# Mixer B of a two-layer encoder: one more dense step ahead of the first transposes, query transposes ahead of the next logits, inverse roots item by item

## The chip, the cores and the metric

The kernel runs on one core of a Trainium2 chip. The metric is the device time of one execution in microseconds (us); the time of a kernel is the median of its runs. Engines are named as the profile names them: PE is TensorE (PEld its weight loads), DVE VectorE, ACT ScalarE, POOL GpSimd, SP SyncE, which here issues most DMAs.

## What is computed

A trunk of two layers over 512 tokens of width 1024. Each layer projects its input once into everything it needs (8448 columns), runs two attention branches, A and B, and merges them. The change is in branch B: grouped attention with 8 query heads and 2 key heads of 64, whose queries and keys are scaled by an inverse root of their mean square and then rotated.

```python
def rms_head(x, g):
    y = xf * lax.rsqrt(jnp.mean(xf * xf, axis=-1, keepdims=True) + QK_EPS) * g
...
def mixer_b(q, k, v, q_norm_g, k_norm_g):
    q = axial_rope(rms_head(q, q_norm_g), ang_row, ang_col)
    k = axial_rope(rms_head(k, k_norm_g), ang_row, ang_col)
    ...
        logits = jnp.einsum('bqkge,bske->bkgqs', qblk, k) * (HEAD_DIM ** -0.5)
        p = jax.nn.softmax(logits, axis=-1)
        return jnp.einsum('bkgqs,bske->bqkge', p, v)
```

Each layer ends with two output projections, a gated sum, one more projection and a layer norm. Everything is float32; dense products are made of three products of rounded parts (high by high, high by low, low by high).

## The kernel before

**The order of the program.** Every engine runs its own instructions in the order in which the program emits them, so the order is written by hand. Per layer there are two generators: `main` (preparation and mixer B, then mixer A, lines 1320 to 1326) and `fill` (all remaining dense products, lines 1328 to 1332). `weave` (line 857) alternates them: each `yield 1` of `main` gives 1.1 credits, and each whole credit lets `fill` emit one dense step. A dense step is either half of a 128x512 output tile (12 matmuls of 512 columns, `feature_unit`) or one 128-token block (24 matmuls of 256 columns, `token_mms`). After each dense step `tick` runs jobs that have come due (`run_later`) and splits one piece of a later weight chunk into its parts: a rounding copy on ACT (line 175) and a subtraction on DVE (line 176).

**Mixer B.** It has 16 items per layer, each two heads of one 128-query block. For item i, `pipeline` (line 671) emits:

- `Q(i)`: two PE transposes of the rotated queries into a PSUM bank (line 616), a copy of the high part on ACT (line 618) and a subtraction for the low part on DVE (line 619).
- `L(i)`: four PE matmuls that make 128x1024 logits (line 632), a maximum on DVE (line 634), a small multiplication by the query factors (line 637), two exponentials on ACT (line 640), a reciprocal and two scalings on DVE (lines 642 and 644).
- `T(i)`: eight PE transposes of the scaled exponentials (line 666) and an eviction of 128x1024 on ACT (line 668).
- `V(i)`: 16 matmuls with the values and a copy on DVE (line 658).

Before the loop come `Q(0)`, `Q(1)`, one `yield 1`, `L(0)` and two times `yield 1`. In the loop the order is `T(i)`, `L(i+1)`, `Q(i+2)`, a yield, `V(i)`, a yield. Mixer A uses the same `pipeline` with `Q` set to None.

**The inverse roots of the queries.** `b_steps` (line 565) calls `q_sums` four times per layer, for (ch, rp) = (0,0), then (0,1) and (1,0) one after the other, then (1,1): squares on ACT (line 475) and a sum on DVE (line 476) into 8 of 32 columns of the tile `qn`. After the fourth, `q_roots` calls `first_root` for all 32 columns: one DVE instruction (line 479), and a power of -1/2 on POOL (line 480). The keys use the same function on 8 columns (tile `nst`). At the first `L`, `q_factors` (line 555) corrects all 32 roots by five small DVE instructions (lines 507 to 510 and 560); the maximum of `L(0)` is emitted behind them.

**PSUM.** Four banks "b" are handed out first in, first out (`B1`). Each dense output tile, each `Q` and each `V` takes one; the next user's first matmul waits until the eviction of the former one is done. In layer 0 the job `rows_` (line 418), which fills two banks from `b<-g,g` matmuls and evicts them on ACT (line 423), and then `bias_rows` (line 251) come due in the tick of the last dense step before `T(0)`. The banks are taken there in the order 3 and 0 (`rows_`), 1 (`bias_rows`), and the dense tile of that step has bank 2.

Of the kernel before, what the change touches and what calls it, by code (L numbers as in the profile page):

```python
# [38 lines left out]
def trunk_kernel(ctx, tc, x, c, rel_table, ln_g, ln_b, w_ada, b_ada, w_in, b_gate,  # L39
# [432 lines left out]
    def square_sums(xq, v):  # L472

        sq = tmp4("s")
        act.activation(sq[:, 0:512], xq, AF.Square)
        dve.tensor_reduce(out=v, in_=sq[:, 0:512].rearrange("p (g d) -> p g d", d=64), op=ADD, axis=AX.X)

    def first_root(v, y):
        dve.tensor_scalar(v, v, 1.0 / 64, 1e-6, op0=MUL, op1=ADD)
        pool.tensor_tensor(out=y, in0=v, in1=mhalf.to_broadcast([128, v.shape[1]]), op=OP.pow)  # L480
# [43 lines left out]
    def k_rotate(st):  # L524

        kn = st["kn"] = small.tile([128, 3, 8], F32, tag="nst", name=fresh("nst"))
        square_sums(st["xk"], kn[:, 0])
        first_root(kn[:, 0], kn[:, 1])
        (a_, b_), sq = rope_parts(st["xk"], 4, 2, 0, 1)
        st["km"] = sq[:, 0:512].rearrange("p (r h d) -> p r h d", r=4, d=64)  # L530
        dve.tensor_add(st["km"], a_, b_)
        G.put(st["xk"])

    def k_scale(st):

        v, y, t = (st["kn"][:, j] for j in range(3))
        newton(v, y, t)
        for rp in range(2):
            kd = st["kd", rp] = G.get()
            kdv = kd.rearrange("p (r h e d) -> p r h e d", r=2, h=2, e=2)  # L540
            for r2 in range(2):
                r = 2 * rp + r2
                dve.tensor_tensor(out=kdv[:, r2], in0=st["km"][:, r, :, None, :].to_broadcast([128, 2, 2, 64]),
                                  in1=y[:, 2 * r:2 * r + 2][:, :, None, None].to_broadcast([128, 2, 2, 64]), op=MUL)

    def q_sums(st, ch, rp):
        if "qn" not in st:
            st["qn"] = small.tile([128, 3, 32], F32, tag="qn", name=fresh("qn"))
        at = 16 * ch + 8 * rp
        square_sums(st["xq", ch, rp], st["qn"][:, 0, at:at + 8])  # L550

    def q_roots(st):
        first_root(st["qn"][:, 0], st["qn"][:, 1])

    def q_factors(st):
        if "qf" not in st:
# [5 lines left out]
    def q_rotate(st, ch, rp):  # L562
        st["qd", ch, 2 * rp], st["qd", ch, 2 * rp + 1] = rope_q(st.pop(("xq", ch, rp)), 2 * rp)

    def b_steps(st):

        k_rotate(st)
        yield
        k_scale(st)
        q_sums(st, 0, 0)  # L570
        yield
        b_keys(st)
        q_rotate(st, 0, 0)
        yield
        q_sums(st, 0, 1)
        q_sums(st, 1, 0)
        yield
        while ("xq", 1, 1) not in st:
            yield
        q_sums(st, 1, 1)  # L580
        q_roots(st)

    def b_prepare(st, rest):
        for _ in st["steps"]:
# [10 lines left out]
    def b_keys(st):  # L595
        for kv in range(2):
            o = B1.get()
            for r in range(4):
                k = st["kd", r // 2].rearrange("p (r h f) -> p r h f", r=2, h=2)[:, r % 2, kv]
                pe.transpose(o[:, 128 * r:128 * r + 128], k, idn)  # L600
            ks = G.get(F32R)
            act.activation(ks, o, AF.Copy)
            dve.tensor_tensor(out=ks[64:128], in0=o[64:128], in1=ks[64:128].bitcast(F32), op=SUB)
            B1.put(o)
            st["ks", kv] = ks
        G.put(st["kd", 0], st["kd", 1])

    def mixer_b(st, ys):
# [41 lines left out]
        def V(i):  # L650
# [8 lines left out]
            B1.put(o)  # L659

        yield from pipeline(len(subs), Q, L, T, V, lambda i: True, st["more"])

    def transpose_p(p):
# [7 lines left out]
    def pipeline(n, Q, L, T, V, need, more=()):  # L671
        if Q:
            Q(0)
            if n > 1:
                Q(1)
        yield 1
        while not need(0):
            yield "need"
        L(0)
        yield 1  # L680
        yield 1
        for i in range(n):
            T(i)
            if i + 1 < n:
                while not need(i + 1):
                    yield "need"
                L(i + 1)
            if Q and i + 2 < n:
                Q(i + 2)
            yield 1  # L690
            V(i)
            if more:
                more.popleft()()
            yield 1
# [5 lines left out]
    def mixer_a(st, hf, ys, more=()):  # L700
# [90 lines left out]
        def need(i):  # L791
            k, pr, pp = subs[i]
            return all(("k", g, hf, pr) in st for g in ((1, 2) if k else (0,)))

        yield from pipeline(len(subs), None, L, T, V, need, more)
        for h in range(4):
            G.put(st.pop(("b0", hf, h)))
# [491 lines left out]
    for l in range(DEPTH):  # L1289
        st = {"more": deque()}  # L1290
        st["steps"] = b_steps(st)
        if l == 0:
            start_layer0(st)
# [107 lines left out]
```

## Time and profile before

| | us |
|---|---|
| median of three runs | 1209.2 (1207.27 to 1209.75) |
| the profiled execution | 1208.29 |
| its span, from the first to the last instruction | 1206.5 |
| PE busy | 1164.3 |
| DVE busy | 674.6 |
| ACT busy | 530.9 |
| POOL busy | 51.6 |

Times in the rows count from the start of the span. Mixer B lies at about 70 to 240 us in layer 0 and 645 to 820 us in layer 1. The profile's granted clock is 1.00 where TensorE runs at 2.4 GHz and 0.5 where it runs at 1.2 GHz.

### The profile page before, as it was taken

What the parts mean: (1) busy time and instruction counts of PE and PEld (TensorE: products, weight loads), DVE (VectorE), ACT (ScalarE), POOL (GpSimd) and SP (SyncE); (2) the same over time, 40 slices, a digit from 0 to 9 for tenths busy, and PEclk for the clock granted to TensorE, in tenths of its full rate; (3) what the DMA queues carried; (4) which work ended last, traced back from release to release, by engine and by line L of the source; (5) the groups of instructions that cost most, each with busy time, mean ns of one, the idle gap of its engine ahead of it and who ended that gap; (6) DMA issues with size and microseconds to landing.
All of it is one profiled execution on the core that took longest, in us unless ns stands there. A gap on an engine that the chain in (4) does not pass through costs nothing.

```text
span 1206.5 us, 19164 instructions
## 1 busy us (share of the span) xinstructions
PE 1164.3 (97%) x7491; PEld 996.7 (83%) x7491; DVE 674.6 (56%) x1576; ACT 530.9 (44%) x1112; POOL 51.6 (4%) x79
## 2 busy tenths in 40 slices
PE   6889999999999999999989899999999999999996
PEld 6878888888887787888989788888888778888896
DVE  6776665555455355336755566754433532943477
ACT  2355545444454454323374445444544454532320
POOL 0021000001000000000001001001000000000000
PEclk9999999999999999999999999999999999999998
DMA  9934434446352233234422335435332322333331
GB/s 280 285 115 135 139 96 127 130 140 176 109 155 88 70 122 105 90 103 154 163 73 71 95 102 152 139 93 177 102 100 67 106 72 94 123 99 102 125 106 70
DMA packets 161314, 146.31 MB, mean 121 GB/s; under 512 B 8942, under 2 KB 149078, under 8 KB 161224
## 3 DMA queue, kind: packets, MB, share of 16 engines
q1 hardware_dynamic: 159176, 139.71, 37.8%
q0 software_dynamic: 2048, 5.38, 1.9%
q8 instruction: 59, 0.97, 0.3%
q14 instruction: 31, 0.25, 0.1%
HBM read 134.87 MB, written 8.62 MB: 119 GB/s over the span
## 4 chain that ended last, share of the span: by engine, by line
PE 83%; DVE 8%; ACT 3%; DMA 2%; issue 1%; SPq 1%; POOL 1%; DVEq 0%; ACTq 0%
PE b L90 71%; PE L L90 6%; PE T L666 5%; DMA raw<-in_w_ada_dram 2%; DVE acc L283 1%; POOL qn L480 1%; DVE wl L176 1%; PE T L90 1%; DVE bst L634 0%; ACT s L640 0%; ACT g L951 0%; PE b L616 0%; DMA s<-in_w_in_dram 0%; SPq L1002 0%; DVE g L1255 0%
## 5 line engine op out<-in xcount | busy, mean ns | idle before, releaser
L176 DVE TENSOR_TENSOR wl<-raw,wh 128x512 fp32r<-128x512 f32 x304 | 205.6, 687 | 296.7 <-ACT wh L175 296.7
L90 PE MATMUL b<-uh,wh 128*128 128x512 f32 x768 | 309.8, 403 | 0.8 <-ACT wh L175 0.5
L90 PE MATMUL b<-uh,wl 128*128 128x512 f32 x768 | 299.6, 390 | 1.0 <-DVE wl L176 0.8
L90 PE MATMUL b<-ul,wh 128*128 128x512 f32 x768 | 300.0, 391 | 0.0
L175 ACT ACTIVATE wh<-raw 128x512 fp32r<-128x512 f32 x304 | 180.1, 623 | 32.7 <-issue 24.8
L90 PEld LDWEIGHTS b<-uh,wh 128*128 128x128 f32 x768 | 144.1, 188 | 42.6 <-issue 12.0
L90 PEld LDWEIGHTS b<-uh,wl 128*128 128x128 f32 x768 | 144.2, 188 | 33.0 <-DVE wl L176 1.8
L90 PEld LDWEIGHTS b<-ul,wh 128*128 128x128 f32 x768 | 144.3, 188 | 26.7
L90 PE MATMUL b<-wh,uh 128*128 128x256 f32 x416 | 122.0, 293 | 0.5 <-DVE qst L619 0.5
L90 PE MATMUL b<-wl,uh 128*128 128x256 f32 x416 | 118.0, 284 | 0.0
L90 PE MATMUL b<-wh,ul 128*128 128x256 f32 x416 | 117.7, 283 | 0.0
L668 ACT ACTIVATE pt<-T 128x1024 f32<-128x1024 f32 x64 | 65.4, 1021 | 79.9 <-PE T L666 79.9
L741 ACT ACTIVATE s<-s,ast 128x256 f32<-128x256 f32 x128 | 63.5, 498 | 78.0 <-DVE ast L736 73.9
L283 DVE SCALAR_TENSOR_TENSOR acc<-raw,sc,acc 128x256 f32<-128x256 f32 x168 | 81.3, 484 | 9.7 <-DMA raw<-in_w_ada_dram 4.6
L90 PEld LDWEIGHTS b<-wh,uh 128*128 128x128 f32 x416 | 79.9, 192 | 5.3 <-issue 3.2
L90 PEld LDWEIGHTS b<-wl,uh 128*128 128x128 f32 x416 | 80.1, 192 | 0.1
L90 PEld LDWEIGHTS b<-wh,ul 128*128 128x128 f32 x416 | 80.0, 192 | 0.0
L90 PE MATMUL b<-g,wh 128*128 128x512 f32 x256 | 79.2, 390 | 0.0
L666 PE MATMUL T<-idn,s 128*128 128x128 f32 x512 | 67.2, 274 | 7.2 <-DVE s L644 6.5
L90 PE MATMUL b<-wh,g 128*128 128x256 f32 x384 | 71.4, 284 | 0.7 <-DVE g L1194 0.5
L640 ACT ACTIVATE s<-L,bst,qn 128x512 f32<-128x512 f32 x64 | 49.3, 774 | 51.1 <-DVE bst L637 51.0
L666 PEld LDWEIGHTS T<-idn,s 128*128 128x128 f32 x512 | 59.1, 141 | 13.9 <-DVE s L644 7.2
(177 smaller groups left out, 1610.8 us busy)
## 6 DMA issues: line engine op xcount, KB each, us to landing
raw<-in_w_in_dram SPq DMA_DIRECT2D x126, 512.0 KB, 4.2
raw<-in_w_ada_dram SPq DMA_DIRECT2D x96, 256.0 KB, 3.5
raw<-in_w_o_dram SPq DMA_DIRECT2D x16, 512.0 KB
g<-in_x_dram SPq DMA_DIRECT2D x16, 256.0 KB, 5.9
vph<-g SPq DMA_DIRECT2D x16, 256.0 KB, 2.1
g<-vph SPq DMA_DIRECT2D x16, 256.0 KB, 5.7
g<-frow SPq DMA_DIRECT2D x32, 128.0 KB, 3.2
raw<-in_w_pa_dram SPq DMA_DIRECT2D x8, 512.0 KB, 3.4
```

The lines of the kernel that those rows point to most:

```text
L90: pe.matmul(o, l, r, start=start, stop=stop, skip_group_check=True)
L175: act.activation(hi[:, d], raw[:, s], AF.Copy)
L176: dve.tensor_sub(lo[:, d], raw[:, s], hi[:, d].bitcast(F32))
L283: dve.scalar_tensor_tensor(a, raw[:, k], col, a, op0=MUL, op1=ADD)
L480: pool.tensor_tensor(out=y, in0=v, in1=mhalf.to_broadcast([128, v.shape[1]]), op=OP.pow)
L640: act.activation(p[:, 512 * e:512 * e + 512], lg[:, 512 * e:512 * e + 512], AF.Exp, scale=f[:, e:e + 1], bias=sm[:, 0, e:e + 1], accum_out ...
L666: pe.transpose(t[:, 128 * j:128 * j + 128], p[:, 128 * j:128 * j + 128], idn)
L668: act.activation(pt, t, AF.Copy)
L741: act.activation(p4[:, e, b], p4[:, e, b], AF.Exp, bias=sm[:, e, b:b + 1], accum_out=s_t[:, rb, e, 1:2])
```

## The change

Three edits. In `pipeline`, a kernel with a `Q` (mixer B alone) yields three times instead of twice between `L(0)` and `T(0)`, and `Q(i+2)` is emitted between `T(i)` and `L(i+1)` instead of behind `L(i+1)`. In `q_sums`, `first_root` is called for the 8 columns just summed, so four times per layer on 8 columns instead of once on 32; `q_roots` goes.

```diff
         square_sums(st["xq", ch, rp], st["qn"][:, 0, at:at + 8])
-
-    def q_roots(st):
-        first_root(st["qn"][:, 0], st["qn"][:, 1])
+        first_root(st["qn"][:, 0, at:at + 8], st["qn"][:, 1, at:at + 8])
...
         q_sums(st, 1, 1)
-        q_roots(st)
...
         L(0)
-        yield 1
-        yield 1
+        for _ in range(3 if Q else 2):
+            yield 1
         for i in range(n):
             T(i)
+            if Q and i + 2 < n:
+                Q(i + 2)
             if i + 1 < n:
                 while not need(i + 1):
                     yield "need"
                 L(i + 1)
-            if Q and i + 2 < n:
-                Q(i + 2)
             yield 1
             V(i)
```

## Rows read from the trace of the kernel before

**Rows 1.** The page, busy time, share of the span and instructions of each engine.
```profile
PE 1164.3 (97%) x7491; PEld 996.7 (83%) x7491; DVE 674.6 (56%) x1576; ACT 530.9 (44%) x1112; POOL 51.6 (4%) x79
```
**Rows 2.** Waits of PE over the span: total us, times, longest us.
```profile
PE T L666 <- DVE s L644: 6.5, 2, 4.4
...
PE b L90 <- DVE qst L619: 0.8, 3, 0.4
```
**Rows 3.** Timeline of PE, layer 1: start us, us, what, idle before and releaser.
```profile
662.00 0.28 PE L90 MATMUL b<-wh,uh 128*128 128x256 f32 x1
...
664.88 0.28 PE L90 MATMUL b<-wh,uh 128*128 128x256 f32 x1
...
667.63 0.28 PE L90 MATMUL b<-wh,ul 128*128 128x256 f32 x1
672.34 1.53 PE L666 MATMUL T<-idn,s 128*128 128x128 f32 x8 [4.43 <-DVE s L644]
...
676.37 0.28 PE L90 MATMUL b<-wh,uh 128*128 128x256 f32 x1
```
**Rows 4.** Windows in layer 1: length, busy us by engine, granted clock, DMA.
```profile
666.00:672.00 6.00, 1.91 (x16) 1.71 (x15) 2.60 (x9) 3.35 (x7) 0.13 (x1) 1.00 0.00 0
672.00:676.00 4.00, 3.66 (x15) 3.17 (x16) 2.29 (x5) 2.12 (x4) 0.00 (x0) 0.61 0.38 115
```
**Rows 5.** Timeline of PE, layer 0, around the first transposes.
```profile
80.43 0.39 PE L90 MATMUL b<-uh,wh 128*128 128x512 f32 x1
...
83.15 0.39 PE L90 MATMUL b<-uh,wh 128*128 128x512 f32 x1
...
87.59 0.27 PE L255 MATMUL b<-idn,g 128*128 128x128 f32 x1
89.92 1.09 PE L666 MATMUL T<-idn,s 128*128 128x128 f32 x8 [2.06 <-DVE s L644]
...
91.92 0.47 PE L90 MATMUL b<-uh,wh 128*128 128x512 f32 x1
```
**Rows 6.** Timeline of DVE, layer 1, before, during and after the power on POOL.
```profile
654.79 1.27 DVE L476 TENSOR_REDUCE qn<-s 128x8 f32<-128x512 f32 x2
...
661.33 0.68 DVE L176 TENSOR_TENSOR wl<-raw,wh 128x512 fp32r<-128x512 f32 x1
666.16 0.19 DVE L507 TENSOR_TENSOR qn<-qn 128x32 f32<-128x32 f32 x1 [4.15 <-POOL qn L480]
```
**Rows 7.** Groups of POOL by line and shape: xcount, busy us, mean ns, idle before.
```profile
L480 POOL TENSOR_TENSOR qn<-qn,mhalf 128x32 f32<-128x32 f32 x2 | 10.9, 5428 | 25.2 <-DVE qn L479 25.2
...
L480 POOL TENSOR_TENSOR nst<-nst,mhalf 128x8 f32<-128x8 f32 x2 | 4.1, 2029 | 34.9 <-DVE nst L479 34.9
```
**Rows 8.** Timeline of DVE, layer 0, the last sums and the first correction.
```profile
75.49 1.27 DVE L476 TENSOR_REDUCE qn<-s 128x8 f32<-128x512 f32 x2
...
77.28 0.68 DVE L476 TENSOR_REDUCE qn<-s 128x8 f32<-128x512 f32 x1
...
83.72 0.19 DVE L507 TENSOR_TENSOR qn<-qn 128x32 f32<-128x32 f32 x1 [2.16 <-POOL qn L480]
```
**Rows 9.** Timeline of ACT, layer 0, behind the exponentials of L(0).
```profile
90.04 1.05 ACT L423 ACTIVATE g<-b 24x512 f32<-24x512 f32 x2
```
**Rows 10.** Timeline of ACT, layer 1, an eviction of T.
```profile
692.73 1.03 ACT L668 ACTIVATE pt<-T 128x1024 f32<-128x1024 f32 x1 [2.89 <-PE T L666]
```
**Rows 11.** All copies of line 618 on ACT: xcount, shortest, median, longest ns, first, last.
```profile
L618 ACT ACTIVATE qst<-b x32: 369/378/383, 76.7 to 800.1; 128x256 fp32r<-128x256 f32 x32
```
**Rows 12.** Timeline of DVE: a maximum and a subtraction (layer 1), scalings (layer 0).
```profile
693.59 1.23 DVE L634 TENSOR_REDUCE bst<-L 128x2 f32<-128x1024 f32 x1 [1.37 <-PE L L90]
...
697.79 0.42 DVE L619 TENSOR_TENSOR qst<-b,qst 128x256 fp32r<-128x256 f32 x1
...
183.83 0.88 DVE L644 TENSOR_SCALAR s<-s,bst 128x512 f32<-128x512 f32 x2
```
**Rows 13.** Timeline of PE, layer 0, the transposes that follow those scalings.
```profile
185.64 1.04 PE L666 MATMUL T<-idn,s 128*128 128x128 f32 x8
```

## The prediction

> **What bounds the kernel now.** I read the shares of busy time first: PE is busy in 97% of the span [rows 1], so an edit pays only where PE stands still or runs slowly. The waits of PE tell where that is [rows 2]. The longest entry is the transposes of line 666 waiting for the scaling of line 644: 6.5 us in two places. The three waits for line 619 are dense tiles whose bank was still held by a Q, 0.8 us together. The rest of the argument is the two places of the first entry, which the timeline of PE shows: in layer 1 PE ends its dense step at 667.91 and starts T(0) at 672.34, 4.43 us later [rows 3]; in layer 0 it stands for 2.06 us before 89.92 [rows 5].
>
> The layer-1 gap costs more than its length. Ahead of it the granted clock is 1.00, and in the 4 us after it 0.61, so part of that stretch ran at the lower level [rows 4]. From T(0) to the fourth dense matmul behind it took 676.37 - 672.34 = 4.03 us [rows 3]. The same T, L and Q took 91.92 - 89.92 = 2.00 us in layer 0 [rows 5], and three dense matmuls of 256 columns take 3 x 0.12 (2.88 us for 24 of them [rows 3]), together 2.36. So the slow clock costs 1.67 us. After the 2.06 us in layer 0 no such slowing is seen.
>
> What is late in both places is one chain: power on POOL, five corrections on DVE, maximum, exponentials, scaling, T. In layer 1 DVE stood 4.15 us for the power [rows 6], in layer 0 2.16 [rows 8].
>
> **The roots by items.** The power took 5.43 us on 32 columns and 2.03 on 8 [rows 7]; each layer gets four of the latter. In layer 1 the second and third sums end at about 655.4 and 656.1 [rows 6], so their powers take POOL from about 655.7 to 659.8; the fourth then starts where the long one did, 5.43 before 666.16, at 660.7. The chain gets shorter by 5.43 - 2.03 = 3.40 us, and T(0)'s data is ready at 672.34 - 3.40 = 668.94. In layer 0 POOL is a queue: the second, third and fourth sums end at about 76.2, 77.1 and 78.6 [rows 8], with the added DVE instruction of some 0.2 us behind each; the second power starts at about 76.45, the third and fourth wait for it, and the last ends at 76.45 + 3 x 2.03 + 0.05 = 82.6. The correction began at 83.72 [rows 8], so the gain there is only 1.1 us: data ready at 88.8. The three added DVE instructions a layer cost PE nothing: DVE waits for POOL behind them. Behind the powers on POOL nothing is due until the bias loads, tens of microseconds later; SP's queue isn't passed.
>
> In the long power of layer 1, DVE's subtraction of line 176, with two inputs in SBUF, took 0.68 us and ended at 662.01, when POOL still had 4 us to go [rows 6, 7]. The Trainium skill (SBUF — State Buffer, section Who interferes with whom) says that such a DVE instruction and a GpSimd instruction that reads SBUF exclude each other for the whole instruction. By that, with POOL at work without a break in layer 0, the subtraction ahead of the correction would start only when the last power ends, the correction 0.7 us later, and the whole gain would be 6.6 us instead of 7.3. The trace doesn't agree, so I take 7.3.
>
> **One more dense step.** The step is moved, not added: fill has one step less later. In layer 1 it is 24 matmuls of 256 columns, 664.88 - 662.00 = 2.88 us [rows 3]. It is the second half of a tile whose bank is already taken, and its weights were split before L(0), so it waits for nothing. PE reaches T(0) at 667.91 + 2.88 = 670.8, 1.9 us after the data is ready. The gap goes, and the slow clock with it: 4.43 + 1.67 = 6.10 us. The roots alone would have left 1.0 us of it, the step alone 1.5.
>
> In layer 0 the step is 12 matmuls of 512 columns, 83.15 - 80.43 = 2.72 us [rows 5], but it starts a new output tile and takes a bank: the free ones are then in the order 3, 0, 1, so it gets bank 3, which the first `rows_` job has just filled. That bank's eviction on ACT (line 423) stands in ACT's queue behind the exponentials of L(0): two of them run from 90.04 to 91.09, so the first ends at about 90.57 [rows 9]. All of this moves with the chain, 1.1 us earlier: 89.5. PE is at that point at 87.86 [rows 5]. So a wait for a bank, 1.6 us, takes the place of the 2.06 us at T(0). After it the step takes 2.72, T(0) starts at 92.2 and waits for nothing. The gain in layer 0 is 2.06 - 1.64 = 0.42 us. Its bounds: 2.06 if the bank comes free in time, and -0.65 if the chain isn't shorter at all there. The lower clock isn't expected, because 2.06 us of idle time had none.
>
> Moved along with the step is its tick: one weight piece on ACT and DVE, queued behind L(0)'s exponentials and ahead of T(0)'s eviction. ACT is idle there, so nothing.
>
> **Q ahead of L.** The same instructions in another order. On PE, L(i+1) starts 0.14 us later. On DVE the maximum now stands behind Q's subtraction, which waits for Q's copy on ACT, which waits for the eviction of T. An example: the eviction runs from 692.73 to 693.76 [rows 10], the copy takes 0.38 [rows 11], the subtraction 0.42 [rows 12], so the maximum starts at 694.5 instead of 693.59: 0.9 us later, with exponentials, scaling and T(i+1) behind it. What covers it is the time from the end of the first scaling to T. For the tightest items it is 185.64 - (183.83 + 0.49) = 1.32 us [rows 12, 13]; four of the 30 items other than the two first have 1.31 to 1.35, the next 2.05, the others 2.6 and more. In the tight ones DVE had a queue, and there the subtraction costs only its own 0.4. So 0.9 is covered everywhere: 0 us. On the gain side, Q's bank comes free about 3 us sooner, so the waits for line 619 go: 0.8 us [rows 2]. It could be as little as 0 if another eviction is then the last.
>
> **The sum.** 6.10 + 0.42 + 0.8 = 7.3 us off the profiled execution's 1208.29, so 1201.0; the median lies 0.9 above that execution, so 1201.9. What I can't cost is that fill stands one step further ahead in all that follows, so other evictions and splits meet at the transposes; from the waits in the rows (0.8 us for three) I bound this by 1.5 us to either side and take 0.
>
> **The rivals.**
> - *The bank is free in time in layer 0.* The 2.06 us go as a whole: 1200.2. The order of ACT speaks against it.
> - *The sums wait for POOL.* If a sum into other columns of `qn` were made to wait until POOL has read its own, the powers in layer 0 come one after each sum and the last ends at about 84.4. The bank is then free at 91.3, PE stands 3.4 us, and layer 0 loses 1.4: 1203.7, and 1205.4 with the lower clock. Layer 1 stays as forecast. Against it: the columns don't overlap.
> - *The shared port,* as above: 1202.6. The row on line 176 speaks against it.
> - *The shift wakes other waits* by 1.5 to 5 us: 1203.4 to 1206.9. Few of PE's waits in the middle are over half a microsecond, which speaks against it.
> - *It does nothing:* what I read as one chain has a second, equally late releaser in layer 1, and the gap only changes its name: about 1208. The chain is gapless from POOL to PE, which speaks against it.
> - *Slower: Q's subtraction holds up the maximum.* Place: all 30 further items. With a delay d, PE loses the sum of d less the cover. From the covers above that is nothing up to 1.3 us, 1.5 at 1.7 us, 7.0 at 2.8 us and 15.2 at 3.3 us. So it decides from about 2.8 us on, where it has eaten the 7.3; at 3.3 the time is 1209.2 - 7.3 + 15.2 = 1217. It would take ACT being 2 us late with T's eviction again and again; in the example it starts when T ends.
>
> **How the numbers follow.** Forecast 0.55, bank free 0.11, sums waiting 0.07, port 0.03, other waits 0.14, nothing 0.06, slower 0.04. Differences under 0.2% (2.4 us) are about what a measurement of this kernel can't tell from no change. Faster by more than that (under 1206.8) are the first four and most of the fifth: 0.88; within: 0.08; slower: 0.04. The range reaches from the bank being free together with favourable shifts (1200.2 less 1.2) to the sums waiting with the lower clock (1205.4): 1199.0 to 1205.5. It leaves out part of the other waits, nothing, and slower.
>
> **What would show it.** In the changed kernel's trace: four powers of about 2.0 us on POOL per layer; T(0) of layer 1 with no idle time before it, and granted clock 1.00 there; in layer 0 a wait of a dense matmul for the eviction of line 423, of about 1.6 us, ahead of T(0); no more waits for line 619; each maximum after the first begins 0.4 to 0.9 us later after its T. I'm wrong if T(0) of layer 1 still waits, if many later T wait for line 644, or if the time comes out within 2.4 us of before.

## The result and the profile after

| | before | changed kernel |
|---|---|---|
| median, us | 1209.16 (1207.27 to 1209.75) | 1199.01 (1198.05 to 1199.13) |
| profiled execution, us | 1208.29 | 1199.13 |
| its span, us | 1206.5 | 1197.0 |
| PE busy, us | 1164.3 | 1163.0 |

The ratio is 0.9921, 95% interval 0.9909 to 0.9933: 10.15 us faster, where 7.3 were forecast. The time lies 0.01 us inside the lower edge of the range (1199.0). That it lies inside is luck: measured once more (last experiment but one), the same kernel took 1198.22.

In the kernels with roots item by item, the lines named in the rows stand three lower than before (T is line 663, its eviction 665, Q's transposes 613, its subtraction 616, the maximum 631, the scaling 641, the transposes of the layer norm 944).

The waits of PE in the changed kernel, the same view as [rows 2] (total us, times, longest us). The waits of T for the scaling are gone, and those of dense tiles for Q's subtraction too. New is one wait for line 423; those for the subtraction of line 176 were 0.8 us before.

```profile
PE b L944 <- ACT g L1271: 6.0, 4, 1.8
...
PE b L90 <- DVE wl L176: 1.7, 2, 0.9
...
PE b L90 <- ACT g L423: 0.6, 1, 0.6
```

The timeline of PE in layer 0, where [rows 5] showed 2.06 us of idle time ahead of T: the wait now stands before the dense step, and T follows the step without any.

```profile
86.81 0.27 PE L255 MATMUL b<-idn,g 128*128 128x128 f32 x1
87.69 0.50 PE L90 MATMUL b<-uh,wh 128*128 128x512 f32 x1 [0.60 <-ACT g L423]
...
90.55 1.03 PE L663 MATMUL T<-idn,s 128*128 128x128 f32 x8
```

In layer 1, where [rows 3] showed 4.43 us, T(0) comes without a wait, and the next T 8.7 us later. The windows there (length, busy us by engine, granted clock, DMA) have the clock at 1.00, against 0.61 in [rows 4].

```profile
668.15 1.04 PE L663 MATMUL T<-idn,s 128*128 128x128 f32 x8
...
676.86 1.03 PE L663 MATMUL T<-idn,s 128*128 128x128 f32 x8
```
```profile
664.00:668.00 4.00, 4.00 (x35) 4.00 (x35) 2.27 (x5) 2.81 (x7) 0.00 (x0) 1.00 0.19 66
668.00:672.00 4.00, 4.00 (x26) 3.52 (x25) 2.00 (x3) 2.31 (x4) 0.00 (x0) 1.00 0.66 197
```

**Two stages as a ruler.** Times of whole executions spread by 1 to 3 us. Two stretches of the trace are steadier: layer 0 from the first transposes of the keys (68.07 us in the changed kernel) to the first transposes of the layer norm (596.72), and layer 1 from the first transposes of the keys (645.05) to the start of the last dense matmul (1185.95). In three traces of the changed kernel or of one that differs from it only on POOL they agree within 0.04 us (layer 0: 528.65, 528.69 and 528.66; layer 1: 540.90 each time). Below they serve to tell where a kernel gains.

| kernel | layer 0, us | layer 1, us | median, us |
|---|---|---|---|
| before | 531.89 | 547.88 | 1209.16 |
| changed | 528.65 | 540.90 | 1199.01 |
| step alone | 533.91 | 545.36 | 1207.53 |
| roots alone | 529.84 | 542.53 | 1200.27 |
| Q ahead alone | 530.62 | 548.79 | 1207.33 |
| step and roots | 530.32 | 543.57 | 1202.10 |
| roots and Q ahead | 528.55 | 542.54 | 1199.21 |
| step and Q ahead | 532.45 | 542.70 | 1202.72 |
| changed, bank free | 527.76 | 540.91 | 1196.68 |
| changed, four steps | 529.02 | 540.99 | 1199.59 |
| changed, maximum twice | 536.25 | 544.81 | 1210.42 |

The change takes 3.24 us from layer 0 and 6.98 from layer 1, 10.2 together, about as the medians do. In the two profiled executions 0.8 us more came from the stretch before the keys, and 1.5 us were lost in the layer norm of layer 0, so that their spans differ by 9.5; the last experiment on the changed kernel itself shows that the loss in the layer norm is chance.

### The profile page after: what moved, and what is told of

It is laid out like the page before. It is cut to its first block, busy times and chain, and to the rows that moved or that the text cites. A ratio compares the mean times of both kernels' runs of the same rounds, so it can differ in the third digit from the quotient of the medians.

```text
span 1197.0 us, 19187 instructions
## 1 busy us (share of the span) xinstructions
PE 1163.0 (97%) x7491; PEld 998.2 (83%) x7491; DVE 675.4 (56%) x1582; ACT 531.1 (44%) x1112; POOL 54.0 (5%) x85
## 4 chain that ended last, share of the span: by engine, by line
PE 88%; DVE 6%; ACT 2%; DMA 1%; issue 1%; SPq 1%; POOL 0%; DVEq 0%; ACTq 0%
PE b L90 75%; PE L L90 6%; PE T L663 5%; DVE acc L283 1%; PE T L90 1%; DMA raw<-in_w_ada_dram 1%; PE b L613 1%; DVE wl L176 1%; ACT g L948 0%; DMA s<-in_w_in_dram 0%; SPq L999 0%; DVE g L1252 0%; DVE g L1258 0%; ACT g L1271 0%; DVE wl L1023 0%
## 5 line engine op out<-in xcount | busy, mean ns | idle before, releaser
L90 PE MATMUL b<-pt,g 128*64 128x128 f32 x1024 | 70.0, 279 | 0.0
L90 PEld LDWEIGHTS b<-pt,g 128*64 128x64 f32 x1024 | 54.6, 136 | 17.7 <-issue 13.7
```

The source lines that it names most:

```text
L90: pe.matmul(o, l, r, start=start, stop=stop, skip_group_check=True)
```

## The experiments

The median of before was measured anew with each group: 1208.95 us for the first four, 1207.55 for the next four, 1207.71 for the three after them, 1208.22 for the last. Time differences below are against the one of the same group.

### The third step alone

```diff
         L(0)
-        yield 1
-        yield 1
+        for _ in range(3 if Q else 2):
+            yield 1
```

> Only the third dense step ahead of T(0). Theory A (the gain of the change is the two waits of T(0) and the slow clock behind the one in layer 1, each part of the change working through the chain from the power on POOL): the power of 5.43 us stays, so in layer 1 T(0) still waits about 1.5 us (4.43 less a step of 2.88) and the clock stays at 1.00 behind it, a gain of 2.88 + 1.67 = 4.5 us; in layer 0 the step waits about 2.7 us for the bank that line 423 evicts, against 2.06 us at T(0) before, a loss of 0.65 us. Together 3.9 us faster. Rival B (most of what went beyond the forecast comes from the shift of all dense steps by one): 1 to 2 us more than that, so 5 to 6 us faster.

Measured: 1207.53 us, ratio 0.9994 (0.9984 to 1.0003): no difference that can be told. T(0) of layer 1 waits 1.54 us, as expected, but the stage there gains 2.5 us and not 4.5. Layer 0 loses 2.0: the step waits 2.79 us for the bank, and the matmuls behind it run at the lower clock (timeline of PE, and a window that begins in that wait, with the granted clock third from the end):

```profile
89.58 0.79 PE L90 MATMUL b<-uh,wh 128*128 128x512 f32 x1 [2.79 <-ACT g L423]
90.17 0.63 PE L90 MATMUL b<-ul,wh 128*128 128x512 f32 x1
90.60 0.63 PE L90 MATMUL b<-uh,wl 128*128 128x512 f32 x1
```
```profile
88.00:92.00 4.00, 2.42 (x6) 1.94 (x7) 3.28 (x8) 3.05 (x7) 0.29 (x1) 0.65 0.10 25
```

And whoever takes a bank behind a Q now waits for Q's subtraction, 4.5 us in all against 0.8 before [rows 2]: two dense tiles in layer 0 (1.58 and 0.29 us), and in layer 1 the matmuls of two V (1.32 and 1.29). So the step alone gives neither theory A's 3.9 us nor rival B's 5 to 6: it wakes waits that neither theory had.

### The roots alone

```diff
         square_sums(st["xq", ch, rp], st["qn"][:, 0, at:at + 8])
-
-    def q_roots(st):
-        first_root(st["qn"][:, 0], st["qn"][:, 1])
+        first_root(st["qn"][:, 0, at:at + 8], st["qn"][:, 1, at:at + 8])
...
         q_sums(st, 1, 1)
-        q_roots(st)
```

> Only the roots item by item. Theory A: the three powers that queue on POOL in layer 0 take 1.6 us each as in the changed kernel, so the chain there is 2.2 us shorter and the 2.06 us wait of T(0) goes; in layer 1 it is 3.8 us shorter (5.43 to 1.64), T(0) waits about 0.6 us, and the clock stays at 1.00 behind it: 2.06 + 3.8 + 1.67 = 7.5 us faster. By the forecast's own sizes (2.03 us a power) it would be 1.1 + 3.4 + 1.67 = 6.2 us. Rival B (the shift of the steps carries the rest): the same 7.5 at most, and the step adds more than 2 us to it in the full change.

Measured: 1200.27 us, ratio 0.9931 (0.9916 to 0.9946), 8.7 us faster; the stages give 2.05 and 5.35, together 7.4. T(0) waits 0.64 us in layer 1 and not at all in layer 0. Theory A's size holds by the stages. This one edit is worth most of the change.

### Q ahead of L alone

```diff
             T(i)
+            if Q and i + 2 < n:
+                Q(i + 2)
             if i + 1 < n:
                 while not need(i + 1):
                     yield "need"
                 L(i + 1)
-            if Q and i + 2 < n:
-                Q(i + 2)
```

> Only the query transposes ahead of the next logits. Theory A: the waits of dense tiles for line 619 go, 0.8 us faster, and T(0) waits as before in both layers (2.06 and 4.43 us) with the slow clock behind the second. Rival B (the order of Q is worth what went beyond the forecast): 2 to 3 us faster. Rival C (Q's subtraction holds up the maximum by 0.9 us and the covers of T don't suffice): no gain, and waits of later T for line 644.

Measured: 1207.33 us, ratio 0.9988 (0.9978 to 0.9997), 1.6 us faster. Layer 0 gains 1.27 us, and the waits for line 619 are gone. In layer 1 T(0) waits 4.42 us as before; there the clock was low for longer than in [rows 4] (0.55 and 0.59 in two windows of 4 us one after the other, the first of which begins in the wait), and that stage was 0.9 us longer in this execution:

```profile
668.00:672.00 4.00, 2.01 (x10) 2.01 (x11) 2.26 (x5) 2.74 (x8) 0.00 (x0) 0.55 0.20 66
672.00:676.00 4.00, 4.00 (x19) 3.61 (x18) 1.81 (x3) 1.65 (x3) 0.00 (x0) 0.59 0.46 131
```

No T waits for the scaling but the two first, so C falls. The 2 to 3 us of B don't show in the stages; the interval of the times alone (0.4 to 2.7 us) would not exclude them.

### The step and the roots, Q behind L

The first two edits together.

> The third dense step and the roots item by item, with the query transposes left behind the logits. Theory A: both waits of T(0) go; in layer 0 the step waits 0.6 us for its bank, in layer 1 nothing waits: 1.46 + 4.43 + 1.67 = 7.6 us faster, and the 0.8 us of line 619 stay in some form. Rival B (the order of Q is worth 2 to 3 us): the same 7.6, and the full change is 2 to 3 us faster than this kernel. Rival: the shift by one step is worth 1 to 2 us by itself, then 9 us faster without the order of Q.

Measured: 1202.10 us, ratio 0.9945 (0.9929 to 0.9962), 6.9 us faster: slower than the roots alone. Both stages are behind those of the roots alone, by 0.5 and 1.0 us, though T(0) waits nowhere. What is late instead is Q's subtraction, for two dense tiles in layer 0 and two V in layer 1, as with the step alone (waits of PE):

```profile
PE b L90 <- DVE qst L616: 4.5, 4, 1.6
```

Putting Q ahead takes 1.67 us from layer 0 and 2.67 from layer 1 on top of this, 4.3 us, where alone it took 1.3 and nothing. So theory A falls by its 0.8 us for line 619; rival B is right that the order of Q is worth over 2 us here, but it is so only behind the step. The third rival, 9 us without the order of Q, falls.

### The roots and Q ahead, without the step

> The changed kernel without the third dense step (roots item by item and Q ahead of L stay). If the step is needed for the two waits of T(0): layer 1 keeps the 0.6 us that the roots alone left, layer 0 nothing, and 8.5 us faster than before (7.7 of the roots alone and 0.8 for line 619), 1 to 2 us slower than the changed kernel. Rival (the step's shift wakes as many waits for line 619 as it removes elsewhere, and the order of Q only mends that): this kernel is as fast as the changed one within 1 us, and has no wait for line 619 and none for line 423.

Measured: 1199.21 us, ratio 0.9932 (0.9917 to 0.9947), 8.3 us faster. By the stages the step on top of this is worth 1.64 us in layer 1 (0.6 us of waiting at T(0) and 0.7 us for an eviction in mixer A go with it) and -0.10 in layer 0, less than the 2 us that rival B of the roots alone asked for. The medians of this kernel and of the changed one (1199.21 and 1199.01) don't show it, and by them alone the rival would hold. The layer norm of layer 0, where the changed kernel's first trace lost 1.5 us and this one didn't, is large enough to hide it; that it did so in the executions without a trace is not shown.

### The bank free for the third step

```diff
-        later(8, rows_)
+        later(9, rows_)
...
-        later(6, lambda: bias_rows(rows, 1))
+        later(7, lambda: bias_rows(rows, 1))
```

> The changed kernel with the two jobs that fill three banks in layer 0 due one tick later, so that the third dense step finds a free bank. Theory (the wait of a dense tile for the eviction of line 423, 0.6 us, is all that is left of the layer-0 gap): that wait goes, nothing takes its place, and the kernel is 0.6 us faster than the changed one. Rival (another wait takes its place, at T(0) or at Q(2) for a bank of those jobs): 0, and the wait shows at another line.

Measured: 1196.68 us (1196.53 to 1196.99), ratio 0.9912 (0.9897 to 0.9927), the lowest median here. The wait for line 423 is gone and nothing takes its place: the jobs' matmuls come behind the step, and T right behind them.

```profile
87.34 0.39 PE L90 MATMUL b<-uh,wl 128*128 128x512 f32 x1
87.57 1.88 PE L90 MATMUL b<-g,g 128*128 128x512 f32 x4
89.29 0.27 PE L255 MATMUL b<-idn,g 128*128 128x128 f32 x1
```

The stage gains 0.89 us, and layer 1 is as in the changed kernel. The medians differ by 2.3 us. The layer norm, 29.45 us here and 30.95 in the changed kernel's first trace, is of the size of the rest; whether it is the cause in the executions without a trace is not shown.

### Four steps

> The changed kernel with a fourth dense step ahead of T(0). Theory (one step covers the chain, and T(0) has 2 us to spare in layer 1 and 3.6 in layer 0; a further one only moves work): no gain at T(0), the same time within 1 us apart from waits that the shift wakes or lays at dense tiles. Rival (the shift of the dense work itself is worth something per step): 1 us or more faster once again.

`range(3 if Q else 2)` with 4 in place of 3. Measured: 1199.59 us, ratio 0.9935 (0.9920 to 0.9950). T(0) gains nothing, layer 1 is the same within 0.1 us, and layer 0 loses 0.4: in place of two waits for a split (1.7 us) there is a single one of 2.4. The rival falls: a further step is worth nothing.

### The maximum three times over

```diff
             dve.tensor_reduce(out=sm[:, 0], in_=lg.rearrange("p (e k) -> p e k", e=2), op=OP.max, axis=AX.X, negate=True)
+            dve.tensor_reduce(out=sm[:, 0], in_=lg.rearrange("p (e k) -> p e k", e=2), op=OP.max, axis=AX.X, negate=True)
+            dve.tensor_reduce(out=sm[:, 0], in_=lg.rearrange("p (e k) -> p e k", e=2), op=OP.max, axis=AX.X, negate=True)
```

> The changed kernel with the maximum of the logits taken three times over, two times 1.2 us more on DVE ahead of the exponentials of every item (the result is the same). It doubles the suspected cost of Q ahead of L several times over: each T then comes 2.4 us later than its data now allows. The covers in the changed kernel's trace (from the end of the first scaling to T) are 0.96 to 2.7 us for 24 of 30 items; the sum of 2.4 less the cover is 9 us in layer 0 and 4 us in layer 1. Theory (the cover is what keeps Q ahead of L free of charge, and what is left of it is as read): T waits for line 644's scaling again in both layers and the kernel is about 13 us slower than the changed one, 3 us slower than before. Rival (PE's queue hides more than the cover shows): under 5 us slower than the changed one.

Measured: 1249.30 us, ratio 1.0350 (1.0332 to 1.0367), 50 us slower than the changed kernel and not 13. T waits for the scaling at 22 items, and the rounding copies of line 175, which stand behind the exponentials on ACT's queue, come late too (waits of PE; the two added lines move the line numbers behind them up by two):

```profile
PE T L665 <- DVE s L643: 30.5, 22, 3.4
...
PE b L90 <- ACT wh L175: 4.7, 2, 4.2
PE b L90 <- ACT g L423: 3.1, 1, 3.1
```

The lower clock shows at four places of mixer B and A. It doesn't behind the longest wait for a bank, that of the third step in layer 0 (timeline of PE, and windows from within that wait on, granted clock 1.00):

```profile
90.49 0.50 PE L90 MATMUL b<-uh,wh 128*128 128x512 f32 x1 [3.11 <-ACT g L423]
```
```profile
88.00:92.00 4.00, 1.51 (x7) 1.25 (x8) 2.52 (x7) 3.96 (x10) 0.00 (x0) 1.00 0.10 24
92.00:96.00 4.00, 4.00 (x24) 3.46 (x23) 1.01 (x3) 1.30 (x2) 3.38 (x6) 1.00 0.71 206
```

### The maximum twice

One added line instead of two.

> The changed kernel with the maximum of the logits taken twice, 1.2 us more on DVE per item (the result is the same). Three times over cost 50 us where the sum of delay less cover gave 13. Theory (the covers hold for one item at a time, and what broke was DVE as a whole, which had no idle time left to catch up): with 1.2 us DVE still catches up, T waits for line 644's scaling only at the two or three items with covers about 1 us, and the kernel is 0.5 to 2 us slower than the changed one. Rival (the covers were misread from the start): 10 us or more slower, with waits of T at most items.

Measured: 1210.42 us, ratio to before 1.0020 (1.0007 to 1.0033), against 1199.01 and 1198.22 for the changed kernel: some 12 us slower, as the stages have it (7.6 in layer 0, 3.9 in layer 1). The theory falls by its size. T waits at eight items, 4.5 us together, not at two or three; the first item's longer chain adds 1.3 us to the wait for line 423; waits for splits grow from 1.7 to 3.9; and the lower clock shows in one place of mixer B in layer 0. That is 8.0 us in waits and, as an estimate from the slow stretch of layer 1 before, 1.7 for the clock; the remaining 1.8 of the 11.5 us show in no row. The rival falls by its form: most items still have cover. DVE as a whole still had idle time (windows in mixer B; the busy us of DVE are the third of the five):

```profile
100.00:240.00 140.00, 136.34 (x941) 117.05 (x940) 105.58 (x204) 64.96 (x133) 0.00 (x0) 0.99 0.40 118
680.00:820.00 140.00, 137.01 (x929) 115.25 (x928) 106.20 (x199) 69.37 (x142) 5.05 (x8) 1.00 0.39 119
```

So DVE was late although it was busy for only 76% of these windows (77 and 79% with the maximum three times over). How, the rows of one wait show, 1.54 us for a rounding copy at 171.76: from 158.66 to 168.95 DVE works without a break, with jobs of lines 283, 492 and 501 ahead of the item's subtraction and its two maxima; ACT stands 5.14 us for the maximum, and the copy stands behind the exponentials (timeline of ACT):

```profile
169.07 0.78 ACT L638 ACTIVATE s<-L,bst,qn 128x512 f32<-128x512 f32 x1 [5.14 <-DVE bst L635]
...
171.07 1.15 ACT L175 ACTIVATE wh<-raw 128x512 fp32r<-128x512 f32 x2
```

That this accounts for all of the 12 us is not shown; no run separates it from other readings.

### The first power twice

```diff
         first_root(st["qn"][:, 0, at:at + 8], st["qn"][:, 1, at:at + 8])
+        if (ch, rp) == (0, 0):
+            pool.tensor_tensor(out=st["qn"][:, 2, at:at + 8], in0=st["qn"][:, 0, at:at + 8],
+                               in1=mhalf.to_broadcast([128, 8]), op=OP.pow)
```

> The changed kernel with the power on POOL for the first item of each layer issued twice, the second time into columns that are written over later. In the changed kernel's trace the first power of each layer takes 2.05 us and the three others 1.63 us, while the forecast put 2.03 us for each. Theory (the first of such instructions after other work on POOL is the dear one): the second of the pair, with the same input, takes 1.6 us. Rival (what it takes hangs on the columns or their values): the second takes 2.05 us as the first does. The time is that of the changed kernel within 1 us.

Measured: 1196.82 us in one run. The timeline of POOL has the pair in layer 0 and in layer 1:

```profile
69.30 2.06 POOL L480 TENSOR_TENSOR qn<-qn,mhalf 128x8 f32<-128x8 f32 x1 [3.15 <-DVE qn L479]
71.33 2.03 POOL L553 TENSOR_TENSOR qn<-qn,mhalf 128x8 f32<-128x8 f32 x1
75.28 4.83 POOL L480 TENSOR_TENSOR qn<-qn,mhalf 128x8 f32<-128x8 f32 x3 [1.92 <-DVE qn L479]
```
```profile
644.73 2.05 POOL L480 TENSOR_TENSOR qn<-qn,mhalf 128x8 f32<-128x8 f32 x1 [3.15 <-DVE qn L479]
646.76 1.63 POOL L553 TENSOR_TENSOR qn<-qn,mhalf 128x8 f32<-128x8 f32 x1
```

The second of the pair took 2.03 us in layer 0 and 1.63 in layer 1, with the same input as the first each time. Neither account holds in both layers. Why three powers of a layer take 1.6 us and others 2.0 stays open.

### The changed kernel once more

> The changed kernel once more, unaltered. In its first trace the granted clock fell to its lower level at 622.9 us, amid the transposes of the layer norm of layer 0 (29.45 us from the first to the last of them in the kernel before, 30.95 in the changed one), where PE waits as in the kernel before. Theory (this belongs to the kernel, by where its idle times fall): the stretch is 30.9 us again and the clock falls there again. Rival (it is chance from one execution to the next): it is 29.4 in this one, and the times of the kernel spread by 1.5 us.

Measured: 1198.22 us (1197.02, 1197.52, 1198.92, 1199.40), ratio 0.9924 (0.9908 to 0.9939). The layer norm of layer 0 took 29.43 us here. The windows there, of the first trace and then of this one, have PE idle for the same time with and without the lower clock behind it:

```profile
620.00:624.00 4.00, 2.18 (x15) 1.98 (x14) 1.62 (x6) 2.53 (x6) 0.00 (x0) 0.86 0.52 152
624.00:628.00 4.00, 4.00 (x27) 4.00 (x26) 1.06 (x2) 2.12 (x6) 0.00 (x0) 0.71 0.02 4
```
```profile
619.00:623.00 4.00, 2.19 (x19) 1.99 (x18) 1.29 (x5) 2.54 (x4) 0.00 (x0) 1.00 0.59 190
623.00:627.00 4.00, 4.00 (x36) 4.00 (x35) 1.68 (x3) 3.63 (x11) 0.00 (x0) 1.00 0.01 4
```

The theory falls: this is chance of the single execution, and 1.5 us of the spread of the times.

### The step and Q ahead, one power as before

> The third dense step and Q ahead of L, with one power on all 32 columns as before. Theory (the order of Q is what makes the step worth anything, and the roots are what shortens the chain): the waits for line 619 of the step alone (4.5 us) go; in layer 1 T(0) waits 1.5 us, and the stage from the keys' transposes to the last dense matmul takes 542.5 us (547.9 before, 540.9 in the changed kernel); in layer 0 the step waits 2.8 us for the bank of line 423 with the lower clock behind it, as with the step alone, and the stage from the keys' transposes to the first transposes of the layer norm takes about 532 us (531.9 before). Together 5 to 6 us faster than before, 4 to 5 slower than the changed kernel. Rival (the step and Q make up the change, the roots add little): within 2 us of the changed kernel.

Measured: 1202.72 us, ratio 0.9955 (0.9941 to 0.9969), 5.5 us faster than before. The stages are 532.45 and 542.70 us, with 2.80 us of waiting for the bank in layer 0, the lower clock behind it, 1.53 us at T(0) in layer 1, and no wait for line 619. The theory holds. The roots are worth 3.80 us in layer 0 and 1.80 in layer 1 on top of it.

## Why the prediction was right, and where it was not

**The bound and the two places.** Right. All but the 0.8 us that show in no row, the change gains from idle time of PE and from the slow stretch behind it. PE's busy time differs by 1.3 us, and by 3.1 against the second trace of the changed kernel (1161.2), where the layer norm ran without the lower clock.

**The roots.** Right in kind: the chain from POOL to T(0) got shorter, the fourth power in layer 1 finds POOL idle, and in layer 0 the powers queue. Too small in size. I put 2.03 us for each power, from the row of the keys [rows 7]. In the queue of layer 0 three took 4.83 us, 1.61 each (timelines of POOL and DVE, changed kernel):

```profile
75.88 4.83 POOL L480 TENSOR_TENSOR qn<-qn,mhalf 128x8 f32<-128x8 f32 x3 [3.93 <-DVE qn L479]
```
```profile
75.71 0.68 DVE L476 TENSOR_REDUCE qn<-s 128x8 f32<-128x512 f32 x1
...
76.51 0.69 DVE L176 TENSOR_TENSOR wl<-raw,wh 128x512 fp32r<-128x512 f32 x1
...
80.09 0.69 DVE L176 TENSOR_TENSOR wl<-raw,wh 128x512 fp32r<-128x512 f32 x1 [1.31 <-ACT wh L175]
80.75 0.19 DVE L507 TENSOR_TENSOR qn<-qn 128x32 f32<-128x32 f32 x1
```

So the last ended at 80.71, not at 82.6 (81.8 when counted from this execution's start of the stage, which is 0.8 us earlier). The correction begins at 80.75 without idle time, right behind a subtraction of line 176: in layer 0 POOL no longer comes last, and a still shorter power would gain nothing there. The rows also settle two rivals. The third sum ran from 75.71 to 76.39, when the power of the second had only begun (75.88): the sums don't wait for POOL. And the subtractions with two inputs in SBUF, from 76.51 and from 80.09, took their usual 0.69 us with POOL at work; the second began 0.62 us before the last power ended. The exclusion that the Trainium skill states (SBUF — State Buffer, section Who interferes with whom) isn't seen here either. One reading of the forecast was off, without effect: behind the long power of layer 0 POOL's next work came 9.1 us later, not tens of microseconds.

**The step in layer 1.** Right: no wait at T(0), 2.15 us to spare (1.9 forecast), no slow clock. The stage gains 6.98 us: 4.43, 1.67, 0.7 for an eviction in mixer A that no longer holds PE up, and 0.2 that no row shows. Forecast were 6.10.

**The step in layer 0.** Right in kind, and this was the finest point of the forecast: the wait at T(0) turns into a wait for the bank that line 423 evicts. Its size was 0.60 us and not 1.64, by the faster powers. With one long power it is 2.79 us, as the same sum gave (2.71). So this part gained 1.46 us, not 0.42: the mis-sized term, 1.0 of the 2.9 us that the forecast lacks. What I left out is the price of the bound: at 2.79 us the lower clock came on top, which the forecast excluded up to 2.06 only; behind 3.11 us at the same place, with the maximum three times over, it didn't.

**Q ahead of L.** The delay was right: in the changed kernel the maximum starts 2.87 us after the start of its T (676.86 above, and below), against 1.99 before (the maximum at 693.59 in [rows 12]; its T starts at 691.60), so 0.88 us later where 0.9 was forecast. The timeline of DVE:

```profile
679.39 0.42 DVE L616 TENSOR_TENSOR qst<-b,qst 128x256 fp32r<-128x256 f32 x1 [0.17 <-ACT qst L615]
679.73 1.21 DVE L631 TENSOR_REDUCE bst<-L 128x2 f32<-128x1024 f32 x1
```

The cover was enough: no T waits. Its gain was read too narrowly. The 0.8 us of [rows 2] is what it removes in the kernel before; behind the extra step, the waits it removes are 4.5 us, and it is worth 4.3. The forecast added the parts up as if each met the kernel before. It came out near because the step's new waits and their removal by Q's order cancel, and as the forecast knew of neither, that is luck.

**The other waits.** I bounded what the shift does elsewhere by 1.5 us to either side and took 0. It was a gain of about 1.6: the waits at T in mixer A (0.75 us) and for one split (0.46) went, one for another split (0.87) came, 0.7 went in layer 1, and 0.6 in layer 0 shows in no row. That lies just outside the bound, and is the larger part of the rest of the 2.9 us.

**The slower rival.** It didn't happen, but its price was wrong. I had it decide at a delay of 2.8 us in all. With the maximum twice, 0.9 + 1.2 = 2.1 us, the kernel loses 12 us and is slower than before. The sum of delay less cover treats each item alone, and gives 3.1 us for a delay of 2.1. So the point from which the edit loses lies between 0.9 and 2.1 us, not at 2.8, when the delay is work on DVE, as here. A delay in which DVE only waits, as the rival had it, was not run.

## What to carry to other kernels

Edits that meet in one pipeline don't add: the step is worth 1.5 us with Q ahead and costs 1.5 without it (by the stages, both with the roots item by item), so forecast them in the order in which they are made, each on the waits that the one before leaves. When a step is moved ahead of a wait, ask first which buffer it takes and behind whose work that buffer's eviction stands; moving two small jobs by one step took another 0.9 us off the stage. And cover that is read item by item is an upper bound: on a DVE that was busy for 63 to 65% of mixer B, a further 1.2 us of work per item cost 12 us, where the covers of the changed kernel (the two tightest 0.97 and 1.04 us) left 0.4.

## What the runs showed of the hardware

The lower clock after idle time isn't a fixed price: behind the same wait at T(0) in layer 1 (4.43 and 4.42 us) a stretch of 4 us at 0.61 followed in one execution and two such stretches at 0.55 and 0.59 in another. Nor did the length of the last wait alone decide whether it came: ahead of the third step of layer 0 it came with waits of 2.79 and 2.80 us and not with one of 3.11; T(0) there had none behind 2.06; and with the maximum twice it came with waits of 1.54 and 0.66 us and one matmul between (granted clock 0.58 from 172 to 176). In the layer norm, where PE waits 0.7, 1.7, 1.8 and 1.8 us with some 7 us of work between, it came in one execution of the changed kernel and not in the next. The power on POOL took 2.0 or 1.6 us on 8 columns and 5.4 us on 32; which of the first two it is, the runs don't explain.
